# Two pads in the pools at the right end of SBUF: a hybrid attention and mLSTM diffusion step

## The chip, the cores and the metric

The kernel runs on one core of one Trainium2 chip. The metric is the device time of one execution in microseconds, as the median of several runs. The engines are named as in the profile: PE is TensorE's matmul, PEld its loading of the stationary operand, DVE is VectorE, ACT is ScalarE, POOL is GpSimd and SP is SyncE, which here only issues DMAs.

## The reference

One layer of a diffusion backbone is computed for 128 context tokens and 1024 latent tokens of width 1024, all in float32. Cut to what matters:

```python
def trunk_layer(x, mods, ...):
    h = rmsnorm(x, norm1_w) * (1 + sc1) + sh1
    aq, ak, av, mq, mk, mv, mo, mg = jnp.split(h @ w_in, SPLIT_POINTS, axis=-1)
    ...
    attn_o = attention(aq, keys, vals)          # 8 query heads, 2 key heads of width 64
    ...
    hm, st_f, st_b = mlstm_bidir(heads(mq), heads(mk) * (MLSTM_DK ** -0.5), heads(mv), gates, init_f, init_b)
    ...
    mix = jnp.concatenate([attn_o, hm], axis=-1) @ w_out
    x = x + g1 * mix
    h2 = rmsnorm(x, norm2_w) * (1 + sc2) + sh2
    x = x + g2 * swiglu(h2, w_gu, w_down)       # 1024 -> 2 x 2816 -> 1024
    return x, ak, av, st_f, st_b

def attention(q, k, v):
    ...
        s = jnp.einsum('bqhgd,bkhd->bhgqk', qi, k).astype(F32) * ATTN_SCALE
        p = jax.nn.softmax(s, axis=-1).astype(v.dtype)
        return jnp.einsum('bhgqk,bkhd->bqhgd', p, v)
```

The modulations (shift, scale, gate) come from SiLU of a conditioning vector times `w_ada`. The context keys, values and the final mLSTM states are outputs too.

## The kernel before

The 1152 tokens are nine blocks of 128 (block 0 is the context), and three blocks form a chunk. Most products are made as three matmuls of a high and a low part (`hi*hi`, `hi*lo`, `lo*hi`): the parts are float32r (a 32-bit form that TensorE takes directly) for the projections out of attention and the FFN, and float16 for the input projection.

The work runs in this order. Up to about 60 us the modulations of the first norm are made and the input is normalised (tiles `x3`, weights of `w_ada` in the tiles `aw0_n_k` of the pool `awp`, at the right end). Then come the key, value and gate columns of the input projection, the query columns (pool `qp`), and from about 200 us the four mLSTM heads, woven with attention for the first chunk. From about 500 us the prefill (`prefill`) multiplies the mLSTM part with `w_out` for all nine blocks; the FFN (`gate_up`, `down`) then runs chunk by chunk, with attention for the next chunk woven in, and after it `attn_out` projects that attention and `norm2` prepares the next chunk. The third chunk's FFN has no attention beside it; `down_last` ends the kernel.

The lines that matter below:

- Attention (lines 995 to 1070). Line 1035 makes the scores `S` with a query stack `qT` as the stationary operand and a key stack `kst` as the moving one, six matmuls of 384 columns for each head and block: 384 in all (context blocks have fewer columns). ACT and DVE make `pr`, `ph` and `pl` (lines 1037 to 1042), two DMA transposes turn `ph` and `pl` into `phT` and `plT` (lines 1044 and 1045), and lines 1059 and 1060 multiply these with the values `vs`.
- `out_block` (lines 1147 to 1149) is the projection with `w_out`: moving `whi` or `wlo` of 512 columns, stationary the high and low parts of the input in a tile `mx`. In the prefill `mx` lies in the pool `xp`. In `attn_out` (line 1265) blocks 0 and 2 of a chunk use a tile `mx` in the place of `qT` in the pool `ap`, and block 1 uses `mix_spare`, the end of the two tiles of the key stacks, which the profile shows as `kst`.
- `gate_up` (lines 1315 to 1317) has weights `whi` and `wlo` as the stationary operand and the normalised input `aTh` and `aTl` as the moving one, 384 columns. `down` (lines 1115 to 1117, and 1391 to 1393 in `down_last`) has `hl`, the activations' parts, as the stationary operand and `whi` or `wlo` as the moving one, 512 columns.
- Line 137 is the helper that subtracts a high part from a full value; line 152 makes the high part of a weight from its raw tile.
- `padded_sil` (lines 321 and 322) clears a padded copy of the conditioning on POOL and fills it on DVE; its second tile, `silp2` in the pool `adp`, is the stationary operand of the later modulations (line 341).

SBUF is handed out by pools in two stacks, one from the left end up and one from the right end down. A pool takes the bytes of its tiles, and the next pool of the same side lies behind it. A pool that is opened where an earlier one was closed reuses its bytes, and then an instruction that writes a tile first waits for what still uses the old tiles that it overlaps. On the right side lies `awp` (closed after the first modulations); in its place `hpk` (the values `vs` and the two tiles of the key stacks); next to it first `kvp` and `adp`, `qp` and later, in their place, `ap` (`qr`, `qT`), `ap2` (`pr`, `ph`, `pl`, `phT`, `plT`, `oT`), `ft` (gates `gl` and `gx`, `t2`), `fp` (small tiles of the norms, `y`, `tn`), and `xp`, in whose place `hlp` (`hl`) comes. All weights, `aTh`, `aTl` and the residual `x1` lie in pools of the left side.

A scheduler orders the instructions of each engine when the program is built, from the code's order and priorities.

Of the kernel before, what the change touches and what calls it, by code (L numbers as in the profile page):

```python
# [8 lines left out]
F32 = mybir.dt.float32  # L9
# [10 lines left out]
P = 128  # L20
# [25 lines left out]
def hybrid_step(ctx: ExitStack, tc: tile.TileContext, I: dict, O: dict):  # L46
# [345 lines left out]
    hp = ctx.enter_context(tc.tile_pool(name="hpk", bufs=1, side="right", reuse_waits="tile"))  # L392
# [539 lines left out]

    vs = hp.tile([P, 10, NKV, 2, HD], F16, name="vs")
    big = [hp.tile([P, KD * CT], F32R, name=f"kst{kv}", tag=f"b{kv}") for kv in range(NKV)]
    kst = [t[:, 0 : 2 * (NB + 1) * P].rearrange("p (t n) -> p t n", t=2) for t in big]
    mix_spare = [t[:, 2 * (NB + 1) * P :].rearrange("p (k x) -> p k x", k=4) for t in big]

# [494 lines left out]
    hp = ctx.enter_context(tc.tile_pool(name="hp", bufs=1, reuse_waits="tile"))  # L1432
    ft = ctx.enter_context(tc.tile_pool(name="ft", bufs=1, side="right", reuse_waits="tile"))
    for tag, bufs in (("gl", 1), ("gx", 1), ("t2", 3)):
        ft.tile([P, 512], F32, name=f"lay_{tag}", tag=tag, bufs=bufs)
    fp = ctx.enter_context(tc.tile_pool(name="fp", bufs=1, side="right", reuse_waits="tile"))

    cur, nxt = {}, {}
    cur["x1"], nxt["x1"] = new_x1(0), new_x1(1)
# [108 lines left out]
```

## Time and profile before

| | us |
|---|---|
| median of 3 runs (lowest, highest) | 1574.08 (1573.49, 1574.66) |
| the profiled execution | 1574.08 |
| its span, from the first to the last instruction | 1572.3 |

The profile is of one execution. Its page gives the busy time of each engine and the chain of waits, followed back from the last instruction, with the share of each engine; other views group instructions by line, engine and shape, or list them in order of time, or cut the span into stages. A group's row ends with the busy time, the mean duration in ns and the idle time of the engine before these instructions, with what ended it. Matmuls are pipelined: a matmul's shown duration is longer than the distance to the next matmul's start, so the cost of a stream of matmuls is read from start to start.

### The profile page before, as it was taken

The page shows a single profiled execution, that of the slowest core. Times are in us where ns is not written, and L with a number is a line of the kernel's source. Part 1 is how long each engine was busy: PE and PEld are TensorE (multiplying, and loading weights), DVE is VectorE, ACT ScalarE, POOL GpSimd, SP SyncE. Part 2 cuts the span into 40 slices and gives each one's busy share as a digit, 9 for nine tenths or more (in the row PEclk, how much of TensorE's full clock was granted, in tenths as well). Part 3 has the DMA queues.
Part 4 walks back from the last instruction along what each step waited for, and adds up shares of the span by engine and source line. Part 5 has one row for each costly group of instructions (what it writes and reads, how often), then busy time and mean ns, then how long its engine had stood idle before and what let it go on. Part 6 is the DMA issues. An engine that isn't in the chain of part 4 may idle for free.

```text
span 1572.3 us, 23397 instructions
## 1 busy us (share of the span) xinstructions
PE 1487.7 (95%) x8539; PEld 1247.3 (79%) x8539; DVE 1022.9 (65%) x2025; ACT 771.8 (49%) x1409; POOL 271.4 (17%) x357
## 2 busy tenths in 40 slices
PE   6899999999999689999999999999999999999996
PEld 3544567676766468898998989989898989999995
DVE  4878554737659576677555677877866585554555
ACT  4754465847656344545432444556552443323332
POOL 0213333322343242100110101000010101001111
PEclk9899999999999799999999999999999999999998
DMA  9664323523556847767555447878763545544441
GB/s 360 186 182 157 97 68 41 121 47 68 114 150 162 265 80 197 184 174 175 154 154 149 147 126 236 195 170 180 179 162 114 168 133 168 161 130 138 143 139 54
DMA packets 387881, 236.91 MB, mean 151 GB/s; under 512 B 170198, under 2 KB 346790, under 8 KB 387766
## 3 DMA queue, kind: packets, MB, share of 16 engines
q1 hardware_dynamic: 385110, 231.84, 54.1%
q10 hardware_dynamic: 2656, 3.58, 1.1%
q8 instruction: 67, 1.10, 0.3%
q14 instruction: 48, 0.39, 0.1%
HBM read 183.79 MB, written 13.26 MB: 125 GB/s over the span
## 4 chain that ended last, share of the span: by engine, by line
PE 77%; DVE 11%; DMA 5%; ACT 4%; issue 2%; SPq 0%; POOL 0%; ACTq 0%; DVEq 0%; POOLq 0%
PE mm L1316 11%; PE mm L1317 11%; PE mm L1315 11%; PE mm L1115 5%; PE mm L1116 5%; PE mm L1117 5%; PE S L1035 3%; PE wi L483 3%; PE wi L485 3%; PE wi L484 3%; PE mm L116 2%; PE mm L1147 1%; PE mm L1148 1%; PE mm L1149 1%; PE po L1060 1%
## 5 line engine op out<-in xcount | busy, mean ns | idle before, releaser
L152 ACT CAST whi<-raw 128x1024 fp32r<-128x1024 f32 (+1 forms) x216 | 222.3, 1029 | 411.0 <-PE mm L1316 156.5
L137 DVE TENSOR_TENSOR wlo<-raw,whi 128x1024 fp32r<-128x1024 f32 (+1 forms) x216 | 260.4, 1206 | 202.9 <-ACT whi L152 202.3
L1316 PE MATMUL mm<-aTl,whi 128*128 128x384 f32 x1056 | 355.7, 337 | 2.7 <-DVE aTl L137 2.7
L1317 PE MATMUL mm<-aTh,wlo 128*128 128x384 f32 x1056 | 354.3, 336 | 0.0
L1315 PE MATMUL mm<-aTh,whi 128*128 128x384 f32 x1056 | 353.3, 336 | 0.0
L137 POOL TENSOR_TENSOR hl<-tn,hl 128x384 fp32r<-128x384 f32 x66 | 84.4, 1279 | 840.0 <-ACT hl L1338 748.3
L1316 PEld LDWEIGHTS mm<-aTl,whi 128*128 128x128 f32 x1056 | 198.5, 188 | 3.9 <-DVE aTl L137 3.3
L1315 PEld LDWEIGHTS mm<-aTh,whi 128*128 128x128 f32 x1056 | 198.1, 188 | 0.6
L1317 PEld LDWEIGHTS mm<-aTh,wlo 128*128 128x128 f32 x1056 | 198.4, 188 | 0.0
L1116 PE MATMUL mm<-wlo,hl 128*128 128x512 f32 x372 | 145.7, 392 | 0.0
L1115 PE MATMUL mm<-whi,hl 128*128 128x512 f32 x372 | 144.3, 392 | 0.0
L1117 PE MATMUL mm<-whi,hl 128*128 128x512 f32 x372 | 143.4, 392 | 0.0
L483 PE MATMUL wi<-ipair,hT 128*128 128x384 f16 (+2 forms) x408 | 135.6, 335 | 1.7 <-ACT hT L507 1.2
L484 PE MATMUL wi<-ipair,hT 128*128 128x384 f16 (+2 forms) x408 | 135.6, 335 | 0.0
L485 PE MATMUL wi<-ipair,hT 128*128 128x384 f16 (+2 forms) x408 | 132.1, 335 | 1.0 <-DVE hT L137 1.0
L1042 DVE SCALAR_TENSOR_TENSOR pl<-pr,st,ph 128x1152 f16<-128x1152 f32 (+1 forms) x72 | 96.0, 1333 | 31.7 <-ACT ph L1041 31.4
L1037 DVE TENSOR_REDUCE st<-S 128x1 f32<-128x1152 f32 (+1 forms) x72 | 88.9, 1235 | 16.3 <-PE S L1035 16.1
L1038 ACT ACTIVATE pr<-S,st 128x1152 f32<-128x1152 f32 (+1 forms) x72 | 81.3, 1130 | 32.4 <-DVE st L1037 29.3
L1041 ACT ACTIVATE ph<-pr,st 128x1152 f16<-128x1152 f32 (+1 forms) x72 | 83.9, 1165 | 23.8 <-DVE st L1040 6.7
L1035 PE MATMUL S<-kst,qT 128*128 128x384 f32 (+1 forms) x400 | 87.6, 349 | 4.8 <-ACT pr L1038 4.8
L1104 DVE TENSOR_TENSOR t<-mm,gl 128x512 f32<-128x512 f32 x102 | 69.1, 687 | 26.2 <-DMA gl<-g_d 11.5
L1117 PEld LDWEIGHTS mm<-whi,hl 128*128 128x128 f32 x372 | 69.9, 188 | 14.2
(375 smaller groups left out, 2538.4 us busy)
## 6 DMA issues: line engine op xcount, KB each, us to landing
raw<-in_w_gu_dram SPq DMA_DIRECT2D x132, 512.0 KB
raw<-in_w_down_dram SPq DMA_DIRECT2D x60, 512.0 KB
a<-in_w_ada_dram SPq DMA_DIRECT2D x24, 512.0 KB
gl<-g_d SPq DMA_DIRECT2D x36, 256.0 KB
aw<-in_w_ada_dram SPq DMA_DIRECT2D x16, 512.0 KB
iraw<-in_w_in_dram SPq DMA_DIRECT2D x32, 256.0 KB
raw<-in_w_out_dram SPq DMA_DIRECT2D x12, 512.0 KB
x<-in_x_sample_dram SPq DMA_DIRECT2D x11, 512.0 KB
```

Source lines behind the costliest of these rows:

```text
L137: (dve if eng == "dve" else pool).tensor_tensor(out=out, in0=full, in1=hi, op=ALU.subtract)
L152: nc.scalar.copy(hi[:, :n], raw[:, :n])
L483: mm(ps[:, :n], ah, wh[:, k % 2, c0 : c0 + n], start=(k == 0), stop=False)
L484: mm(ps[:, :n], ah, wl[:, k % 2, c0 : c0 + n], start=False, stop=False)
L485: mm(ps[:, :n], al, wh[:, k % 2, c0 : c0 + n], start=False, stop=(k == KD - 1))
L1035: mm(S[:, n, 0:w], qT[:, h, :], kst[kv][:, t, c0 + n * w : c0 + (n + 1) * w], start=(t == 0), stop=(t == 1))
L1115: mm(ps, ah, wh[:, k % 2, :], start=(k == 0), stop=False)
L1116: mm(ps, ah, wl[:, k % 2, :], start=False, stop=False)
L1117: mm(ps, al, wh[:, k % 2, :], start=False, stop=(k == nk - 1))
L1315: mm(ps, wh[:, k, :], th[:, k, :], start=(k == 0), stop=False)
L1316: mm(ps, wh[:, k, :], tl[:, k, :], start=False, stop=False)
L1317: mm(ps, wl[:, k, :], th[:, k, :], start=False, stop=(k == KD - 1))
```

## The change

Two tiles are added that nothing writes or reads: 24 float32, 96 bytes of each partition, behind the key stacks in the pool `hpk`, and 8 float32, 32 bytes, in the pool `fp`.

```diff
     vs = hp.tile([P, 10, NKV, 2, HD], F16, name="vs")
     big = [hp.tile([P, KD * CT], F32R, name=f"kst{kv}", tag=f"b{kv}") for kv in range(NKV)]
+    hp.tile([P, 24], F32, name="lay_hpk")
     kst = [t[:, 0 : 2 * (NB + 1) * P].rearrange("p (t n) -> p t n", t=2) for t in big]
...
     fp = ctx.enter_context(tc.tile_pool(name="fp", bufs=1, side="right", reuse_waits="tile"))
+    fp.tile([P, 8], F32, name="lay_fp")
```

The first pad moves `hpk`'s tiles and every pool behind it down by 96 bytes, the second moves `xp` and `hlp` by 32 more. In the two built programs the tiles start, as bytes past a multiple of 128 (in brackets past a multiple of 256):

| tiles | before | after |
|---|---|---|
| `vs`, `kst0`, `kst1` | 96 | 0 |
| `mix_spare`, the end of the key stacks' tiles | 96 (224) | 0 (128) |
| `qr`, `qT` and `mx` in its place | 96 (96) | 0 (0) |
| `pr`, `ph`, `pl`, `phT`, `plT`, `oT`, `ol` | 96 | 0 |
| `ph`, `pl`, `phT`, `plT` | (96) | (0) |
| `gl`, `gx`, `fw`, `t2`, `jk`, `y`, `tn` | 96 | 0 |
| `kall`, `vall`, `silp2`, `a4` of `kvp` and `adp` | 96 | 0 |
| `cc`, `ss`, `nr0` of `qp` | 32 | 64 |
| `qraw` of `qp` | 64 | 96 |
| `hl`, and `mx` of `xp` | 0 (0) | 0 (128) |
| weights, `aTh`, `aTl`, `x1`, the mLSTM's tiles, `awp` | unchanged | unchanged |

The instructions of the two programs and their order on each engine are the same. The waits differ in one place: `silp2` started exactly where the tile `aw0_0_2` had started, and now its first 96 bytes also overlap the tile `aw0_0_1`, so its memset on POOL and its copy on DVE also wait for the load of `aw0_0_1`. They waited for the load of `aw0_0_2` and for the matmuls on it already.

## The prediction

> **What bounds the kernel now.** I read the page's busy row and its chain of waits first, then the table of stages, because a change of addresses can only act through the work that is already there: it issues nothing of its own.
>
> ```profile
> PE 1487.7 (95%) x8539; PEld 1247.3 (79%) x8539; DVE 1022.9 (65%) x2025; ACT 771.8 (49%) x1409; POOL 271.4 (17%) x357
> PE 77%; DVE 11%; DMA 5%; ACT 4%; issue 2%; SPq 0%; POOL 0%; ACTq 0%; DVEq 0%; POOLq 0%
> ```
> ```profile
> 400.00:560.00 160.00, 136.72 (x838) 102.72 (x837) 107.81 (x272) 88.81 (x224) 56.27 (x84) 0.94 0.64 169
> 560.00:700.00 140.00, 130.74 (x718) 114.24 (x717) 95.04 (x146) 68.78 (x95) 28.85 (x21) 1.00 0.65 163
> 700.00:1000.00 300.00, 298.97 (x1615) 276.11 (x1613) 197.65 (x294) 130.27 (x170) 27.07 (x21) 1.00 0.59 166
> 1000.00:1250.00 250.00, 250.00 (x1414) 230.80 (x1414) 182.24 (x258) 131.59 (x174) 19.39 (x16) 1.00 0.69 165
> ```
> The columns of the stages are busy time of PE, PEld, DVE, ACT and POOL, the granted clock, the DMA share and GB/s. From 700 to 1250 us TensorE is busy 548.97 of 550 us at a granted clock of 1.00. There only a shorter step of the matmul stream saves time; a faster DVE, ACT, POOL or DMA saves nothing. Between 400 and 700 us TensorE stands idle for 32.5 of 300 us, and there a transfer or an instruction on the chain could count.
>
> **The change part by part.** Both programs issue the same instructions in the same order on all five engines. The pads move addresses. Everything in the pools from the key stacks down to the softmax tiles, `t2`, `gl`, `y` and `tn` goes from 96 past a multiple of 128 bytes to 0; `qp`'s tables go from 32 to 64; `hl` and `xp`'s `mx` stay at 0 modulo 128 but go from 0 to 128 modulo 256. And one wait is added, in front of `silp2`. So the question is what an operation costs at 96 and at 0, and the trace holds pairs of that.
>
> *Matmuls with a stationary operand at 96.* The output projection's lines 1147 to 1149 run in the prefill on `mx` of `xp` (offset 0) and in `attn_out` on the spare of `kst` and on `mx` in `qT`'s place (both 96), with the same moving weights and 512 columns. First the prefill, then the two others; the columns are start, duration, engine and line:
>
> ```profile
> 552.70 0.39 PE L1148 MATMUL mm<-wlo,mx 128*128 128x512 f32 x1
> ...
> 554.29 0.39 PE L1149 MATMUL mm<-whi,mx 128*128 128x512 f32 x1
> ...
> 865.16 0.40 PE L1147 MATMUL mm<-whi,kst 128*128 128x512 f32 x1
> ...
> 867.95 0.39 PE L1147 MATMUL mm<-whi,mx 128*128 128x512 f32 x1
> 868.64 0.40 PE L1148 MATMUL mm<-wlo,mx 128*128 128x512 f32 x1
> ...
> 870.99 0.40 PE L1149 MATMUL mm<-whi,mx 128*128 128x512 f32 x1
> ```
> From start to start: 7 steps in 1.59 us at offset 0, 227 ns each; 12 steps in 2.79 us on the spare, 232.5 ns; 10 steps in 2.35 us on `qT`'s place, 235 ns. So offset 96 costs 5.4 and 7.9 ns a matmul. `attn_out` runs twice with 3 blocks, 2 halves and 12 matmuls: 144, of which 48 on the spare. That is 48 x 5.4 + 96 x 7.9 = 1.0 us, all in the stage where TensorE has no idle time.
>
> [...]
>
> *The scores.* Line 1035 has both operands at 96; the rows around it are gate and up products of equal width (384 columns) with both at 0:
>
> ```profile
> 1100.06 0.33 PE L1316 MATMUL mm<-aTl,whi 128*128 128x384 f32 x1
> ...
> 1103.18 1.21 PE L1035 MATMUL S<-kst,qT 128*128 128x384 f32 x6
> 1104.23 0.34 PE L1316 MATMUL mm<-aTl,whi 128*128 128x384 f32 x1
> ```
> ```profile
> L1035 PE MATMUL S<-kst,qT 128*128 128x384 f32 x384 | 83.8, 351 | 4.8 <-ACT pr L1038 4.8
> ```
> 18 steps in 3.12 us are 173.3 ns; the six score products take 1.05 us, 175.0 ns. 384 x 1.7 ns = 0.65 us. The chain gives other score groups 1.06 us, which would make 1.3 us; that the excess has another cause makes it 0. I take 0.65.
>
> *DVE, ACT and POOL.* Pairs of equal shape, the first of each with all operands at 0, the second reading `fl` at 96:
>
> ```profile
> L137 DVE TENSOR_TENSOR wlo<-raw,whi 128x512 fp32r<-128x512 f32 x12 | 8.2, 687 | 18.5 <-ACT whi L152 18.5
> L137 DVE TENSOR_TENSOR aTl<-fl,aTh 128x512 fp32r<-128x512 f32 x12 | 8.3, 692 | 0.0
> L152 ACT CAST whi<-raw 128x512 fp32r<-128x512 f32 x12 | 7.5, 624 | 31.7 <-PE mm L1117 18.2 <-PE mm L1316 12.9 <-DMA raw<-in_w_down_dram 0.5
> L1309 ACT CAST aTh<-fl 128x512 fp32r<-128x512 f32 x18 | 11.2, 624 | 6.1 <-DVE fl L1304 5.8 <-DVE rt L131 0.2
> ```
> ACT: nothing. DVE: 5 ns of 690, under 1%, which may be nothing; at most 1% of DVE's 11% of the chain, 1.7 us, would come back. I take 0 for these engines: where TensorE is saturated it hides them, and without that cover it would be those 1.7 us. `qp`'s move from 32 to 64 goes with them.
>
> *Transfers.* What TensorE waits for from moved tiles, from the table of waits and from the readers of `pl`:
>
> ```profile
> PE mm L116 <- DMA t<-hm_d: 9.4, 1, 9.4
> PE po L1060 <- DMA plT<-pl: 2.0, 2, 1.3
> PE po L1059 <- DMA phT<-ph: 0.9, 1, 0.9
>   PEld L1060: 1.6, 1
>   PEld L1059: 0.2, 1
> ```
> ```profile
> 514.53 5.16 DMA raw<-in_w_out_dram
> 522.46 4.25 DMA t<-hm_d
> 641.86 5.39 DMA plT<-pl
> ```
> On the chain a load into the moved `t2` takes 4.25 us and one into the unmoved `raw`, of twice the size, 5.16 us. Both are latency and queueing more than bytes, so I take 0. The ends are 0 and what the rival below gives.
>
> *The added wait.* `silp2` now also overlaps `aw0_0_1` (load, 512 KB), so its memset on POOL and its copy on DVE wait for that load too.
>
> ```profile
> L341 PE MATMUL mm<-a,silp x192: 379/403/634, 69.9 to 156.7; 128*32 128x256 f32 x192
> L321 POOL MEMSET silp<- x2: 312/312/312, 0.7 to 22.5; 128x256 f32 x2
> L322 DVE COPY silp<-sil x2: 165/170/176, 6.7 to 39.5; 128x16 f32<-128x16 f32 x2
> ```
> Both already wait for the matmuls on `aw0_0_2`, which TensorE runs after those on `aw0_0_1`: the new load has been read by then. The memset starts at 22.5 us, the copy at 39.5, the first matmul on `silp2` at 69.9. Cost 0. Without that cover it is DVE's queue that is late: behind the copy stand the modulations of lines 333 and 336, which the first features need.
>
> Sum: 1.0 + 0.65 + 0 + 0 + 0 = 1.65 us less. The profiled execution took 1574.08 us (span 1572.3, 1.8 around it), which is also the median of the runs, so 1574.08 - 1.65 = 1572.4 us. 0.2% is 3.15 us: below 1570.9 counts as faster and above 1577.2 as slower, about what a measurement of this kernel can tell from no change.
>
> **The rivals.** (a) *The coarser step.* The pairs only compare 96 with tiles at multiples of 512. If what TensorE wants of a stationary operand is a multiple of 256 or 512, then `hl`, which goes from 0 to 128 modulo 256, starts to pay:
>
> ```profile
> L1116 PE MATMUL mm<-wlo,hl 128*128 128x512 f32 x372 | 145.7, 392 | 0.0
> L1115 PE MATMUL mm<-whi,hl 128*128 128x512 f32 x372 | 144.3, 392 | 0.0
> L1117 PE MATMUL mm<-whi,hl 128*128 128x512 f32 x372 | 143.4, 392 | 0.0
> L1392 PE MATMUL mm<-wlo,hl 128*128 128x512 f32 x24 | 9.4, 390 | 0.0
> ```
> 1116 matmuls, and 72 in the last group (lines 1391 to 1393), at 5.4 to 7.9 ns are 6.4 to 9.4 us, the prefill's 216 on `xp`'s `mx` 1.2 to 1.7 more, and the gains above are mostly lost: about 1582 us. It decides from 2.7 ns a matmul (3.15 us / 1188). For it: nothing in the trace excludes it. Against: the spare and `qT`'s place differ modulo 256 (224 and 96), yet pay nearly alike.
>
> (b) *Faster transposes.* `ph`, `pl`, `phT` and `plT` come to multiples of 256. Were the transposes short enough to clear the waits on `phT` and `plT` (2.0 + 1.6 + 0.2, plus a 0.9 us wait of line 1059) and half of the 5.39 us piece of the chain, that is 4.7 + 2.7 = 7.4 us at the most; half of it, 3.7, with the matmuls' 1.65 gives 1568.7 us. It decides from 1.5 us. Against: from 700 us on nobody waits long enough to gain. [...]
>
> (c) *No effect at all*: the pairs differ by stage and neighbours, not by address; 1574.1 us. Against it: the same line, three places.
>
> (d) *The wait bites*: 3.5 us or more at the start, 1578; the order of the matmuls all but excludes it.
>
> **How the numbers follow.** Forecast 0.60, (c) 0.04, both within 0.2%: 0.64. (b) 0.22: faster. (a) 0.12 and (d) 0.02: slower 0.14. The forecast's own range is 1570.0 (all upper ends: 1.0 + 1.3 + 1.7) to 1574.7 (nothing gained, and the runs' upper end). The range of 8 in 10 reaches to 1569.0, into the upper half of (b), and to 1576.0; what is left out is (a), (d) and (b)'s lower part.
>
> **What would show it.** Right: lines 1147 to 1149 after 850 us step at about 227 ns in all three places, the score groups at about 1.04 us, `hl`'s products unchanged, DVE, ACT and landings unchanged. Wrong: `hl`'s lines 1115 to 1117 longer (a); waits on `phT` and `plT` gone and the stage from 560 to 700 us shorter (b); the copy of `silp2` much later than 39.5 us (d).

## The result and the profile after

| | us |
|---|---|
| median of 11 runs before (lowest, highest) | 1573.49 (1570.59, 1575.17) |
| median of 11 runs after | 1577.35 (1574.79, 1583.14) |
| ratio after to before, with its 95% interval | 1.0028 (1.0016 to 1.0040) |
| the profiled execution after, and its span | 1577.87, 1576.1 |

The changed kernel is slower: 1573.49 x 0.0028 is 4.4 us, with bounds of 2.5 and 6.3 us. The prediction had 1572.4 us, between 1569.0 and 1576.0.

The page after the change has the same picture as before. Its busy row and the row of its chain of waits:

```profile
PE 1491.4 (95%) x8539; PEld 1247.5 (79%) x8539; DVE 1022.1 (65%) x2025; ACT 770.5 (49%) x1409; POOL 272.2 (17%) x357
PE 78%; DVE 10%; DMA 5%; ACT 4%; issue 2%; SPq 1%; POOL 0%; ACTq 0%; DVEq 0%; POOLq 0%
```

TensorE is busy 3.7 us longer (1487.7 before), and no other engine moves by more than 1.3 us. So the time is in the matmuls, and the groups by line say in which (lines are one higher than before from line 936 on, two higher from line 1437 on):

```profile
L1117 PE MATMUL mm<-wlo,hl 128*128 128x512 f32 x372 | 147.2, 396 | 0.0
L1116 PE MATMUL mm<-whi,hl 128*128 128x512 f32 x372 | 145.9, 396 | 0.0
L1118 PE MATMUL mm<-whi,hl 128*128 128x512 f32 x372 | 144.9, 397 | 0.0
L1393 PE MATMUL mm<-wlo,hl 128*128 128x512 f32 x24 | 9.5, 394 | 0.0
L1036 PE MATMUL S<-kst,qT 128*128 128x384 f32 x384 | 83.4, 349 | 4.0 <-ACT pr L1039 4.0
```

The three products of `down` on `hl` rise from 392 to 396 or 397 ns. As matmuls overlap (in `down` a product shows 392 ns before, and the next one starts about 228 ns after it), the cost is read from start to start. The last group of the kernel shows it without any wait between. First the kernel before, then after; the first row of each is the first of 192 `gate_up` products, the second is the first and the third is the last of the 72 products of the last `down`:

```profile
1509.32 0.33 PE L1315 MATMUL mm<-aTh,whi 128*128 128x384 f32 x1
...
1542.63 0.39 PE L1391 MATMUL mm<-whi,hl 128*128 128x512 f32 x1
...
1558.76 0.39 PE L1393 MATMUL mm<-whi,hl 128*128 128x512 f32 x1
```
```profile
1512.99 0.34 PE L1316 MATMUL mm<-aTh,whi 128*128 128x384 f32 x1
...
1546.30 0.39 PE L1392 MATMUL mm<-whi,hl 128*128 128x512 f32 x1
...
1562.79 0.40 PE L1394 MATMUL mm<-whi,hl 128*128 128x512 f32 x1
```

The 192 `gate_up` steps take 33.31 us in both, 173.5 ns each. The 71 steps of `down` take 16.13 us before and 16.49 us after: 227.2 and 232.3 ns. Nothing but the start of `hl` differs for them, 0 or 128 bytes past a multiple of 256.

The same can be read in `out_block`, where the moved tiles went both ways. After the change, in the prefill (stationary `mx` of `xp`, from 0 to 128 past a multiple of 256), and then in `attn_out` (the spare of `kst`, from 224 to 128, and `mx` in `qT`'s place, from 96 to 0):

```profile
549.82 0.39 PE L1149 MATMUL mm<-wlo,mx 128*128 128x512 f32 x1
...
552.16 0.39 PE L1149 MATMUL mm<-wlo,mx 128*128 128x512 f32 x1
```
```profile
864.73 0.40 PE L1148 MATMUL mm<-whi,kst 128*128 128x512 f32 x1
...
868.92 0.39 PE L1148 MATMUL mm<-whi,mx 128*128 128x512 f32 x1
...
871.87 0.62 PE L1150 MATMUL mm<-whi,mx 128*128 128x512 f32 x2
```

The prefill's 10 steps take 2.34 us, 234 ns, where they took 227. The spare's 18 steps take 4.19 us, 232.8 ns, as before. The 13 steps on `mx` that follow take 2.95 us, 226.9 ns, where this place took 235.

Over the whole trace, the mean distance between neighbouring starts of a group (distances of over 250 ns left out, 200 ns for products of 384 columns, so that waits and missing records do not count) is:

| products, ns from start to start | count | before | after | us |
|---|---|---|---|---|
| `down` on `hl` | 1116 | 227.89 | 232.51 | +5.2 |
| last `down` on `hl` | 72 | 227.24 | 232.35 | +0.4 |
| prefill `out_block` on `mx` of `xp` | 216 | 228.35 | 232.51 | +0.9 |
| `attn_out` on `mx` in `qT`'s place | 96 | 233.82 | 227.09 | -0.6 |
| `attn_out` on the spare | 48 | 233.12 | 232.79 | 0.0 |
| scores `S` | 384 | 175.66 | 175.91 | +0.1 |
| `gate_up`, nothing moved | 3168 | 173.67 | 173.54 | -0.4 |

The moved groups add up to 5.9 us, inside the 2.5 to 6.3 us of the runs. The spans of the two profiles differ by less, 3.8 us. From the first `gate_up` product to the last `down` product the trace before has 943.8 us, the trace after 946.4 (614.96 to 1558.76, and 616.43 to 1562.79). The steps under 250 ns grow by 4.9 us in that stretch (913.1 to 918.0), the waits of over 0.6 us between products shrink by 2.0 (four with 6.1 us, then three with 4.2), those between from 24.6 to 24.2. The longer products may cover part of these waits, or the waits may differ from run to run; which of the two it is was not shown.

### The profile page after: what moved, and what is told of

Its sections match the earlier page's. It is cut to its first block, busy times and chain, and to the rows that moved or that the text cites. A ratio compares the mean times of both kernels' runs of the same rounds, so it can differ in the third digit from the quotient of the medians.

```text
span 1576.1 us, 23397 instructions
## 1 busy us (share of the span) xinstructions
PE 1491.4 (95%) x8539; PEld 1247.5 (79%) x8539; DVE 1022.1 (65%) x2025; ACT 770.5 (49%) x1409; POOL 272.2 (17%) x357
## 4 chain that ended last, share of the span: by engine, by line
PE 78%; DVE 10%; DMA 5%; ACT 4%; issue 2%; SPq 1%; POOL 0%; ACTq 0%; DVEq 0%; POOLq 0%
PE mm L1317 11%; PE mm L1318 11%; PE mm L1316 11%; PE mm L1116 5%; PE mm L1117 5%; PE mm L1118 5%; PE S L1036 4%; PE wi L485 3%; PE wi L483 3%; PE wi L484 3%; PE mm L1148 2%; PE mm L1149 2%; PE mm L1150 2%; PE mm L116 1%; PE po L1061 1%
```

## The experiments

The question after the traces was whether the slower `hl` products are the cost, and what about `hl`'s place makes them slow. Each experiment moves tiles by pads and issues the same work in the same order on each engine. The three programs with moved weights also have three more semaphore waits, two on DVE and one on ACT (23400 instructions in their profiles instead of 23397); the run with everything at 128 has them too, and its ratio of 1.0001 shows no cost. Times are held against runs of the kernel before on the same chip.

**`hl` back to a multiple of 256.** The changed kernel with a longer second pad:

```diff
-    fp.tile([P, 8], F32, name="lay_fp")
+    fp.tile([P, 40], F32, name="lay_fp")
```

> The changed kernel with one pad longer: 40 floats instead of 8 ahead of hl in the MoE's F-pool, so that hl and the prefill xp's mx start again at a multiple of 256 bytes, as they did before the change; every other pad stays. Theory (TensorE wants an f32r stationary operand at a multiple of 256 bytes): the 1116 down products with hl go back from 232.5 to 227.9 ns from start to start, the 216 prefill out_block products from 232.5 to 228.4; 96 attn_out products keep their gain (234 to 227). Time 0.65 us under the kernel before, a ratio of 0.9996. Rival 1 (another pad or the added wait ahead of the decode silu costs the time, and the slower products only stand beside it): the products go back but the time stays 4 us over before, ratio 1.0025. Rival 2 (the products slow down because of something else in the changed kernel, such as its neighbours in SBUF): they stay at 232.5 ns, ratio 1.003.

Measured: ratio 0.9998 (0.9986 to 1.0009). `down` is back at 227.7 ns, the prefill at 228.8, and the 96 `attn_out` products keep their 227.1. Everything else of the change is still there, the first pad and the added wait included, and costs nothing that can be measured. Rivals 1 and 2 fall.

**Only `hl` moved.** The kernel before with 128 bytes ahead of `hl`:

```diff
     fp = ctx.enter_context(tc.tile_pool(name="fp", bufs=1, side="right", reuse_waits="tile"))
+    fp.tile([P, 32], F32, name="lay_fp")
```

> The kernel before with one pad alone: 32 floats ahead of hl in the MoE's F-pool, so that hl and the prefill xp's mx start 128 bytes past a multiple of 256; nothing else of the change is there, neither the pads of the attention pools nor the added wait. Theory (stationary operand off a multiple of 256): down products 232.5 ns instead of 227.9 (1116 times, 5.1 us), the last group's 72 (0.4 us) and the prefill out_block's 216 (0.9 us): 6.3 us in all, ratio 1.004, and more than the whole change, which had 0.65 us of gain beside it. Rival 1 (another pad or the wait): ratio 1.000, products at 227.9. If the products slow down but the time does not, other work hides them: ratio 1.000 to 1.002.

Measured: ratio 1.0034 (1.0021 to 1.0048), 5.3 us; `down` at 232.3 ns, the prefill at 232.7. This one move costs about as much as the whole change (4.4 us). More was expected, as the change has `attn_out`'s gain beside it; the intervals of the two overlap, so the times do not show that difference.

**All moved operands at multiples of 256.** Both pads are longer, and one is added in `ap` (its first two lines only fix the order of the tiles):

```diff
-    hp.tile([P, 24], F32, name="lay_hpk")
+    hp.tile([P, 56], F32, name="lay_hpk")
...
+    ap.tile([P, NQ, HD], F32, name="lay_qr", tag="qr", bufs=1)
+    ap.tile([P, NQ, P], F32R, name="lay_qT", tag="qT", bufs=1)
+    ap.tile([P, 32], F32, name="lay_ap")
...
-    fp.tile([P, 8], F32, name="lay_fp")
+    fp.tile([P, 40], F32, name="lay_fp")
```

> The changed kernel with its pads made longer, so that every stationary operand that the change touches (kst, vs, qT, hl, mx, and the softmax tiles phT) starts at a multiple of 256 bytes. Theory with a step of 256 for every f32r stationary operand: down products at 227.9 ns, the 144 attn_out products at 227 ns (96 from 234, 48 from 233: 0.9 us gained on before), and if the 384-column score products pay too, 384 of them from 175.7 to 173.5 ns, 0.8 us more: 0.9 to 1.7 us under before, ratio 0.9989 to 0.9994. Rival (the step is 512, not 256, or the second 128 bytes were only by chance the fast ones): attn_out's 48 on the key stack's spare place stay at 233 ns. Rival (one of the other pads costs): ratio 1.0 or above with the products at 227 ns.

Measured: ratio 0.9990 (0.9978 to 1.0001). Both groups of `attn_out` take 226.7 ns, so the spare's 128 past a multiple of 256 was what had kept it slow: the step is not 128. It is not 512 either: by the built programs the spare then starts 256 past a multiple of 512, and so did `hl` in the run with the longer second pad, at 227.7 ns. The scores take 175.5 ns: no 2 ns are gained there.

**A moving operand off.** Up to here only stationary operands of the large groups had been moved. The kernel before, with `aTh` and `aTl` at 128:

```diff
     hp = ctx.enter_context(tc.tile_pool(name="hp", bufs=1, reuse_waits="tile"))
+    hp.tile([P, 32], F32, name="lay_hp")
```

> The kernel before with 32 floats ahead of aTh, aTl and x1 in their pool: the moving operand of the 3168 gate_up products starts 128 bytes past a multiple of 256; no stationary operand moves. Theory (only the stationary operand pays): gate_up stays at 173.7 ns from start to start, ratio 1.000. Rival (any operand that TensorE reads off a multiple of 256 costs about 4.6 ns per 512 columns, 3.5 ns per 384): gate_up at 177 ns, 11 us, ratio 1.007.

Measured: ratio 1.0044 (1.0029 to 1.0058), 6.9 us, and `gate_up` at 175.75 ns, 2.1 ns more on each of 3168 products, 6.6 us. My theory that only the stationary operand pays falls; the rival's 177 ns were too much. In its last group the 192 steps of `gate_up` take 33.71 us (175.6 ns), the 71 of `down` 16.11:

```profile
1513.87 0.34 PE L1315 MATMUL mm<-aTh,whi 128*128 128x384 f32 x1
...
1547.58 0.40 PE L1391 MATMUL mm<-whi,hl 128*128 128x512 f32 x1
...
1563.69 0.39 PE L1393 MATMUL mm<-whi,hl 128*128 128x512 f32 x1
```

**The weights alone off.** `whi` and `wlo` at 128, everything behind them kept in place:

```diff
     wp = ctx.enter_context(tc.tile_pool(name="wp", bufs=1, reuse_waits="tile"))
+    wp.tile([P, 1024], F32, name="lay_raw", tag="raw", bufs=2)
+    wp.tile([P, 32], F32, name="lay_wp")
     hp = ctx.enter_context(tc.tile_pool(name="hp", bufs=1, reuse_waits="tile"))
+    hp.tile([P, 32], F32, name="lay_hp")
```

> The kernel before with 32 floats ahead of the MoE's weight tiles and 32 more ahead of aTh, so that whi and wlo start 128 bytes past a multiple of 256 and aTh, aTl, x1, hl and mx all stay at 0. That moves the stationary operand of the 3168 gate_up products (384 columns) and the moving operand of the 1188 down and 360 out_block products (512 columns). Theory A (every f32r operand off a multiple of 256 costs, the stationary one as much at 384 columns as at 512): gate_up 173.7 to 178 ns (3168 times 4.6 ns, 14.6 us), down 227.9 to about 230.7 (the moving operand's 2.1 ns at 384 columns, times 512/384; 1548 times 2.8 ns, 4.3 us): 19 us, ratio 1.012. Theory B (the stationary operand costs nothing in products of 384 columns, as the 384 score products did not change when theirs moved): gate_up stays at 173.7, down at 230.7, ratio 1.003. Theory C (the moving operand costs only with 384 columns): down at 227.9.

Measured: ratio 1.0072 (1.0054 to 1.0091), 11.3 us. `gate_up` takes 175.84 ns, `down` 232.66. Neither A nor B nor C has these numbers. What they do equal is the price of moving the other operand: `gate_up` pays 2.2 or 2.1 ns, with its stationary or its moving operand at 128 (175.84, 175.75), and `down` 4.8 or 4.6 ns (232.66, 232.51).

**Weights and `aTh` off together.** As the last one, without the pad in `hp`, so that `aTh` and `aTl` lie at 128 as well:

```diff
+    wp.tile([P, 1024], F32, name="lay_raw", tag="raw", bufs=2)
+    wp.tile([P, 32], F32, name="lay_wp")
```

> The kernel before with 32 floats ahead of the MoE's weight tiles alone: whi and wlo start 128 bytes past a multiple of 256, and so do aTh and aTl, which follow them. Both operands of gate_up are off, and the moving one of down and out_block. If the two operands' prices add: gate_up at the value it has with the weights alone off, plus 2.1 ns (6.6 us more than that run). If TensorE pays once for a product that has any operand off: gate_up as with the weights alone off. down as there.

Measured in one run: `gate_up` 173.59 ns, as with nothing moved. Two prices of 2 ns neither add nor hide each other, they vanish. `down`, whose weights are at 128 and whose `hl` is at 0, stays at 232.4. The last group shows both, 192 steps in 33.31 us and 71 in 16.50:

```profile
1512.01 0.34 PE L1315 MATMUL mm<-aTh,whi 128*128 128x384 f32 x1
...
1545.32 0.39 PE L1391 MATMUL mm<-whi,hl 128*128 128x512 f32 x1
...
1561.82 0.40 PE L1393 MATMUL mm<-whi,hl 128*128 128x512 f32 x1
```

So a new theory, R: what counts is how far apart the two operands of a product start, modulo 256. `attn_out` agrees: in both of these runs `mx` (96) and the spare (224) meet weights at 128 and not at 0, and they exchange their times, 233.2 and 233.7 ns where the kernel before has 233.8 and 233.1.

**Smaller distances, one run each.** `aTh` at 64, and `hl` moved by 64:

```diff
+    hp.tile([P, 16], F32, name="lay_hp")
```
```diff
+    fp.tile([P, 16], F32, name="lay_fp")
```

> The kernel before with 16 floats ahead of aTh, aTl and x1: the moving operand of gate_up starts 64 bytes past a multiple of 256. Theory (any start off a multiple of 256 costs the same): gate_up 175.7 ns, as with 128 bytes, about 7 us. Rival (the price goes by the distance, or multiples of 64 are as good): between 173.7 and 174.7 ns, 0 to 3 us.

> The kernel before with 16 floats ahead of hl in the MoE's F-pool: hl and the prefill xp's mx start 64 bytes past a multiple of 256 instead of 0. Theory (any start off a multiple of 256 costs the same): down 232.3 ns, as with 128 bytes, 6 us. Rival (by distance): about 230 ns, 3 us; or more than with 128 (attn_out's 96 products took 233.8 ns from 96 bytes past and the key stack's 48 took 232.8 from 128 past): 233.5 ns, 8 us.

Measured: `gate_up` 173.3 ns, so 64 bytes cost nothing there. `down` 229.1 ns, 1.2 more than at 0. The second expectation misplaces its tile: pools at the right end grow downward, so `hl` started 64 bytes short of a multiple of 256, at 192.

**Everything off, but alike.** Weights, `aTh`, `aTl`, `hl` and the prefill's `mx` all at 128:

```diff
+    wp.tile([P, 1024], F32, name="lay_raw", tag="raw", bufs=2)
+    wp.tile([P, 32], F32, name="lay_wp")
...
+    fp.tile([P, 32], F32, name="lay_fp")
```

> The kernel before with 32 floats ahead of the MoE's weight tiles and 32 ahead of hl: whi, wlo, aTh, aTl, hl and the prefill xp's mx all start 128 bytes past a multiple of 256; both operands of each gate_up, down and prefill out_block product share one remainder. Theory R (what counts is the distance between the two operands' starts modulo 256, not where each starts): gate_up 173.6 ns, down 227.9, prefill out_block 228.4, ratio 1.000, although every one of these operands is off. Only attn_out's change places: with whi at 128 the 96 products with mx at 96 are 224 apart and take 233.2 ns, the 48 with the key stack at 224 are 96 apart and take 233.7, as in the run with both of gate_up's operands off. Theory A (each operand off a multiple of 256 costs by itself): gate_up 175.8 or more, down 232.5 or more, 7 + 6 us, ratio 1.008. If the two operands' prices merely hide each other in gate_up, down stays at 232.5: 6 us, ratio 1.004.

Measured: ratio 1.0001 (0.9987 to 1.0015). `gate_up` 173.6 ns, `down` 227.7, the prefill 228.5; `attn_out` 233.2 on `mx` and 233.7 on the spare. None of these big groups has an operand at a multiple of 256, and none pays. Theory A falls. In the last group, 192 steps in 33.30 us and 71 in 16.14:

```profile
1513.57 0.33 PE L1315 MATMUL mm<-aTh,whi 128*128 128x384 f32 x1
...
1546.87 0.39 PE L1391 MATMUL mm<-whi,hl 128*128 128x512 f32 x1
...
1563.01 0.39 PE L1393 MATMUL mm<-whi,hl 128*128 128x512 f32 x1
```

**The price by distance, one run each.** `hl` at 64 and at 224:

```diff
+    fp.tile([P, 48], F32, name="lay_fp")
```
```diff
+    fp.tile([P, 8], F32, name="lay_fp")
```

> The kernel before with 48 floats ahead of hl: as the pools at the right end grow downward, hl then starts 64 past a multiple of 256 (the run named hl64 had it at 192, 64 short of one). Theory R with a price that depends on the distance alone, not on its sign: down 229.1 ns, as at 192. If the sign counts (96 apart took 233.8 in attn_out, 224 apart 233.1): 230 to 233.8 ns.

> The kernel before with the change's own 8 floats ahead of hl and nothing else: hl 224 past a multiple of 256. Theory R: down as attn_out's products at a distance of 224 (233.1 ns, the key stack before; 233.2, mx with whi at 128), 5.2 ns more than at 0, 1404 products, 7 us. If the price belongs to attn_out's stage and not to the distance: down below 230 ns.

Measured: `down` at 233.3 ns in both. At 224 it pays as `attn_out` does at that distance, so the price belongs to the distance and not to the stage. At 64 it pays in full, where at 192 it had paid a quarter: the sign counts. With all runs, for products of 512 columns:

| start of the stationary less that of the moving operand, modulo 256 | ns from start to start | from |
|---|---|---|
| 0 | 227.9, 227.7; 227.1, 226.7 | `down`, both at 0; both at 128; `attn_out` after the change; with all moved operands at multiples of 256 |
| 64 | 233.3 | `down`, `hl` at 64 |
| 96 | 233.8, 233.7 | `attn_out`, 96 and 0; 224 and 128 |
| 128 | 232.5, 232.7; 232.8 | `down`, 128 and 0; 0 and 128; `attn_out`'s spare after the change, 128 and 0 |
| 192 | 229.1 | `down`, `hl` at 192 |
| 224 | 233.3, 233.1, 233.2 | `down`, 224 and 0; `attn_out`, 224 and 0; 96 and 128 |

For products of 384 columns it is 173.6 at 0, 175.8 at 128 and 173.3 at 192.

**All moved operands at multiples of 256, and `aTh` at 64.** The kernel of the earlier run with all moved operands at multiples of 256, with one pad more:

```diff
     hp = ctx.enter_context(tc.tile_pool(name="hp", bufs=1, reuse_waits="tile"))
+    hp.tile([P, 16], F32, name="lay_hp")
```

> The kernel with all moved operands at multiples of 256, and 16 floats more ahead of aTh, so that gate_up's operands are 192 apart. In the run with that distance alone gate_up took 173.3 ns instead of 173.6 from start to start. If that is the distance's doing: 173.3 ns again, 3168 times 0.3 ns, 1 us less than with all at multiples of 256, ratio to the kernel before 0.998 to 0.999. If it was chance: 173.5 to 173.7 ns and a ratio of 0.999.

Measured: ratio 0.9988 (0.9976 to 0.9999), 1.9 us under the kernel before. `gate_up` is at 173.3 ns again, `attn_out` at 226.7. The repeated 173.3 speaks for the distance, but does not settle it: `down`, whose operands stand as in the kernel before, is also 0.3 to 0.4 ns faster in the two runs with `aTh` at 64 (227.55 and 227.50 ns instead of 227.89). In time this kernel cannot be told from the one without that pad (0.9990).

The steps account for the times of the kernels that were run several times. The sum is the count of each group times its difference to the kernel before:

| kernel | sum of the steps, us | measured, us (interval) |
|---|---|---|
| `hl` alone at 128 | +6.3 | +5.3 (3.3 to 7.5) |
| `aTh` at 128 | +6.6 | +6.9 (4.6 to 9.1) |
| weights at 128 | +13.5 | +11.3 (8.5 to 14.3) |
| all at 128 | 0 | +0.2 (-2.0 to 2.4) |
| moved operands at 0 | -1.0 | -1.6 (-3.5 to 0.2) |
| the same, `aTh` at 64 | -2.2 | -1.9 (-3.8 to -0.2) |

The kernels that were run once have no interval; against the median of the kernel before on the same chip they gave +5.8 us with weights and `aTh` at 128 (sum +6.3), +1.8 with `aTh` at 64 (-1.1), 0.0 with `hl` at 192 (+1.7), +5.5 with `hl` at 64 (+7.5) and +7.9 with `hl` at 224 (+7.5). Runs of the kernel before differ by 7 to 11 us among themselves (1568.93 to 1575.94 on one chip, 1568.66 to 1580.12 on another), so these are read by their steps and not by their times.

## Why the prediction was wrong

**The step that failed** is in the change part by part: `hl` and `xp`'s `mx` "stay at 0 modulo 128 but go from 0 to 128 modulo 256", and the sum has no term for them. The pairs of rows that this rested on compare 96 with 0 against weights at 0. They show that a stationary operand at 96 is slow beside such weights; that 128 is as good as 0 they cannot show, and the prediction itself says so in rival (a). The missing term is 5.2 + 0.4 + 0.9 = 6.5 us, on 1404 products, 1188 of them in `down`, in a stretch where TensorE hardly waits (before, four waits of over 0.6 us, 6.1 of 943.8 us); the forecast's gain on matmuls with 512 columns came from 144.

**Rival (a)**, with a chance of 0.12, names the right rows and the right sign: `hl`'s lines are longer, as it said they would be. Its 5.4 to 7.9 ns a matmul were 4.6, and its 1582 us was 1577.35. Its cause was not right either. It has TensorE want a stationary operand on a multiple of 256 or 512; with weights, `aTh`, `aTl`, `hl` and the prefill's `mx` all at 128, `gate_up`, `down` and the prefill have none there and lose nothing. What decides for these groups is the distance between the starts of the two operands. In the rows of `out_block` and `down` before the change this could not be read: the moving weights were always at 0, so that a place and a distance were the same number. The argument that the prediction set against (a) was none: 224 and 96 are both off a multiple of 256, so that they pay alike says nothing of 128.

**Stationary operand at 96.** The 96 products on `qT`'s place gain 6.7 ns each, where the pair had said 7.9. The 48 on the spare gain nothing instead of 5.4, since the spare goes from 224 to 128, which is as slow. The term of 1.0 us was 0.6.

**The scores.** The term of 0.65 us was nothing: 175.66 and 175.91 ns. The same group of six that was quoted from before takes 1.06 us to the next product after the change, where it had 1.05:

```profile
1104.70 1.22 PE L1036 MATMUL S<-kst,qT 128*128 128x384 f32 x6
1105.76 0.33 PE L1317 MATMUL mm<-aTl,whi 128*128 128x384 f32 x1
```

Before, `kst` is at 224 and `qT` at 96; after, they are at 128 and 0. They are 128 apart both times, so by R nothing should change, and nothing does. But R alone would also have the scores gain 2 ns where both are at 0, as `gate_up` does, and they take 175.5 and 175.8 ns there. Why the scores take the same time at a distance of 128 and at 0 stays open. So R is shown for `gate_up`, `down` and `out_block`, and not for every float32r product. The excess over `gate_up` that the prediction priced did not go with the move, as its own lower end had it; its cause is not known.

**DVE, ACT and POOL at nothing** was right: ACT's cast of `fl` keeps its 624 ns, and DVE's subtraction from `fl` goes from 692 to 685 ns on 12 instructions. In the run with `hl` back at a multiple of 256, where `fl` is moved as well, it takes 693 ns, so neither the 7 ns nor the 5 ns of the prediction's pair is an effect of the place.

```profile
L1310 ACT CAST aTh<-fl 128x512 fp32r<-128x512 f32 x18 | 11.2, 624 | 6.0 <-DVE fl L1305 5.6 <-DVE rt L131 0.2
L137 DVE TENSOR_TENSOR aTl<-fl,aTh 128x512 fp32r<-128x512 f32 x12 | 8.2, 685 | 0.0
```

**Transfers at nothing** was right as far as the times show, and rival (b), with its gain of up to 7.4 us, did not happen. That the loads are latency and queueing more than bytes was an estimate from 4.25 us for 256 KB against 5.16 us for 512 KB; no run takes these times apart. No run shows that a start at a multiple of 256 makes a transpose faster: `plT` still ends waits of TensorE (2.0 and 1.6 us before, 2.2 and 1.2 after), and the piece of the chain on it went from 5.39 to 5.08 us:

```profile
PE mm L116 <- DMA t<-hm_d: 11.5, 1, 11.5
PE po L1061 <- DMA plT<-pl: 2.2, 2, 1.3
PEld L1061 <- DMA plT<-pl: 1.2, 1, 1.2
```
```profile
521.54 4.40 DMA t<-hm_d
642.08 5.08 DMA plT<-pl
```

One sign of (b) did appear: the single wait of 0.9 us on `phT` (line 1059) is gone after the change and in the three experiments with the first pad, while every other profile has it at 0.7 to 0.9 us. Its worth is 0.9 us at the most, and why it went was not shown. The wait on `t<-hm_d` is 2.1 us longer in this profile than before; over the experiments it varies from 9.0 to 11.3 us, without going with either pad.

**The added wait at nothing** was right: the second copy into a padded tile starts at 39.6 us, where it was 39.5. Rival (d) falls, and the kernel with `hl` back in place, which still has that wait, shows it in time. **Rival (c)** falls with the two groups of `out_block` that changed in opposite directions.

```profile
L322 DVE COPY silp<-sil x2: 167/171/175, 6.8 to 39.6; 128x16 f32<-128x16 f32 x2
```

## What to carry to other kernels

Where TensorE is saturated, list for each group of matmuls where both operands start, stationary and moving, before and after a change of layout, and multiply by the count: here 1404 products that lost 4 to 5 ns outweighed 96 that gained 7. A pair of rows that differ in one place prices that place alone; if the other operand never moved in the data, the rule may be about the two together, and moving the other one is the cheapest experiment that tells. In this kernel, with both operands starting alike modulo 256 bytes, `gate_up`, `down` and each place of `out_block` always came within half a nanosecond of the fastest step that the same group had in any run.

## What the runs showed that was not expected

In `down` and `out_block` a float32r product of 512 columns took 226.7 to 228.8 ns from start to start when its operands started alike modulo 256 bytes and 232.3 to 233.8 ns at distances of 64, 96, 128 and 224, with 229.1 ns at 192. At 128 (232.5 and 232.7 ns in `down`), and in `attn_out` at 96 (233.8 and 233.7) and 224 (233.1 and 233.2), it made no difference which of the two was moved; 64 and 192 were tried with one operand only. This does not hold for every product. The scores show no price (175.5 to 175.9 ns at 128 and at 0), and the float16 products of lines 1059 and 1060 (256 columns) do not either: their operands start 128 apart before and after the change and alike with all moved operands at multiples of 256, and the mean step of neighbours is 110.2 ns in all three traces.

No run here shows where the price arises. Weight loads overlap the products (PEld is busy 79% of the span, PE 95%), but a load of `hl` in the last group has the same mean duration of 188 ns before and after the change. What the runs give is its size, 1.2 to 5.4 ns for each product of `down`, by where one operand lies to the other.
